# One forward substitution for both head groups of a gated delta rule, with the steps around it in another order

## The chip, the cores and the metric

The kernel runs on one core of a Trainium2 chip. The core has five engines that work through their own queues of instructions in order: TensorE (PE in the profile, for matmuls; PEld is its weight load), VectorE (DVE), ScalarE (ACT), GpSimd (POOL) and SyncE (SP, which issues the DMAs). An instruction waits on semaphores for what it needs from other engines, and everything behind it in the same queue waits with it. The metric is the device time of one launch in microseconds (us); smaller is better.

## What is computed

A decoder trunk of two layers on 512 tokens of width 1024. Layer 0 mixes tokens by a gated delta rule with six heads beside a cross-attention into 256 memory tokens; then follow an MLP, layer 1 (sliding-window attention) and its MLP. The change lies in layer 0 alone. The reference for it, cut:

```python
def gated_delta_rule(q, k, v, g, beta):
    ...
    L = jnp.where(strict, jnp.einsum('bhnid,bhnjd->bhnij', k_beta, k) * decay, 0.0)
    rhs = jnp.concatenate([v * beta[..., None], k_beta * jnp.exp(g)[..., None]], axis=-1)
    sol = lax.linalg.triangular_solve(L, rhs, left_side=True, lower=True, unit_diagonal=True)
    u, w = sol[..., :DV], sol[..., DV:]
    intra = jnp.where(incl, jnp.einsum('bhnid,bhnjd->bhnij', q, k) * decay, 0.0)
    ...
    def step(state, inp):
        qd, kd, uc, wc, ac, cd = inp
        v_new = uc - jnp.einsum('bhik,bhkv->bhiv', wc, state)
        out = jnp.einsum('bhik,bhkv->bhiv', qd, state) + jnp.einsum('bhij,bhjv->bhiv', ac, v_new)
        state = state * cd[..., None, None] + jnp.einsum('bhik,bhiv->bhkv', kd, v_new)
        return state, out

def mixer_a(h, mem, ...):
    proj = h @ w_in
    qkv = jax.nn.silu(causal_depthwise_conv(qkv, conv_w))
    ...
    o = gated_delta_rule(q, k, v, g, beta)
    o = o * lax.rsqrt(jnp.mean(o * o, axis=-1, keepdims=True) + NORM_EPS) * norm_w
    o = o * jax.nn.silu(z)
    mo = memory_cross_attention(qm, mem, mem_w_kv)
    return jnp.concatenate([o, mo], axis=-1) @ w_o
```

The kernel takes chunks of 128 tokens, so each head has 4 chunks. It needs, for each head and chunk, the inverse of a unit lower triangular matrix of 128 x 128.

## The kernel before

The six heads form two groups of three. The mixer of layer 0 is written as steps, each a function, and the string MIXER_ORDER lists them in the order in which they are written out; run_steps calls them. A letter is the step, the digits are its arguments. The tile framework then sets the final order of each engine's queue from the dependencies, so the order below shows what became of it.

The steps, with the lines of the kernel of before: q (proj_qm) is a projection. E (make_E1, from L339) makes a group's decay matrices: y on VectorE and on GpSimd (L346), two matmuls (L348), an Exp. k (group_kq) projects a head's k and q, runs a short convolution and a Silu over each (conv_silu: y on ScalarE at L356, three products on VectorE at L358, Silu at L360), and forms the products ak (L385) and from them LT, the triangular matrices. v (group_v) projects a head's v and runs the same convolution; w (group_v2) transposes it (vt, L430) and scales it (vr or TT, L431). z (proj_z) projects the gate z. Weights come through wload: a DMA into wr, a rounding cast wh on ScalarE (L87), the remainder wl on VectorE (L88), in few buffers. Most products are three f32r matmuls, of hi with hi, hi with lo and lo with hi.

i (inv_blocks) inverts the 32 x 32 diagonal blocks of a group's twelve matrices, in 48 rows of VectorE: the blocks go by DMA from LT to DRAM (dl, L442) and back with a block on each row (ld, L444), then 31 pairs of a product (tmp, L454) and a subtraction from X (L456), then X goes through DRAM (dx, L458) into TT (L461). j (inv_join) makes whole inverses from the blocks: transpose of TT into U (L467), products ipp, ip2, ip3 (copies Pf at L475 and L476), then iqp and iq for the 64 x 64 half. i and j run once for each group.

c (group_chunk) is a chunk of the scan for three heads: kt (a transpose of k), ks and qs (with the state S), R = v - ks on VectorE (L526), tr = U R (L532), vn, ds (L538, for the next state S), od. o (chunk_out) norms the chunk's output: sso, then f, with a power on GpSimd (L568), and a product with z in res (L573). n (z_norm) applies Silu to z (L657, ScalarE) and multiplies by the norm weights (L659, GpSimd). m is the memory attention in three parts, scores (msc), turn (mpt) and values (mov), which a pipeline (push, flush) spreads over later units. f (close_tile) transposes the mixed rows; W and p (wo_open, wo_tile) are the output projection; L (ln_tile) is the layer norm.

In before, both groups' steps interleave with projections as fillers: group 0 is inverted (i0, j0) while v and w are projected, its chunks c00 to c03 run among the v and w of group 1, and c10 to c13 among W and p.

Of the kernel before, what the change touches and what calls it, by code (L numbers as in the profile page):

```python
# [11 lines left out]
F32 = mybir.dt.float32  # L12
# [37 lines left out]
def trunk(ctx: ExitStack, tc: tile.TileContext, xT, xn, memT, wk, wq, wv, wqm, wz, wmk, wmv, wo0, wo1, up, dn,  # L50
# [47 lines left out]
    wa_stack = ExitStack()  # L98
    wpool[0] = wa_stack.enter_context(tc.tile_pool(name="wa", bufs=3))

    def feature_major(ps, w, mov_hi, mov_lo):
        hi, lo = w
        for k in range(KT):
            mh, ml = mov_hi(k), mov_lo(k)
            T.matmul(ps, hi[:, k, :], mh, start=(k == 0), stop=False)
            T.matmul(ps, hi[:, k, :], ml, start=False, stop=False)
            T.matmul(ps, lo[:, k, :], mh, start=False, stop=(k == KT - 1))

# [179 lines left out]
    def dt_(shape, tag, bufs=2, dt=F32):  # L288
        return dp.tile(shape, dt, tag=tag, name=nm(tag), bufs=bufs)
# [45 lines left out]
    GH = 3  # L335
    NU = GH * 4

    def make_E1(gi):
        E1 = dt_([P, NU, P], "E1")  # L339
        for hl in range(GH):  # L340
            h = GH * gi + hl
            ps = smt("E1")
            psv = ps.rearrange("p (c i) -> p c i", c=4)
            for i, eng in enumerate((V, G)):
                gm = dt_([P, 4, P], "y", dt=F32R)
                eng.tensor_tensor(gm, triu[:, :].unsqueeze(1).broadcast_to([P, 4, P]),  # L346
                                  fr(gsp[i])[:, h * 4:h * 4 + 4].unsqueeze(2).broadcast_to([P, 4, P]), op=ALU.mult)
                T.matmul(ps, slow, gm.rearrange("p c i -> p (c i)"), start=(i == 0), stop=(i == 1))  # L348
            dst = E1[:, hl * 4:hl * 4 + 4, :]
            V.tensor_tensor(dst, psv, mtri[:, :].unsqueeze(1).broadcast_to([P, 4, P]), op=ALU.add)  # L350
            A.activation(dst, dst, AF.Exp)
        E1s[gi] = E1

    def conv_silu(ps, ch, dst):
        y = dt_([P, 512], "y")
        A.activation(y, ps, AF.Identity, scale=convw[:, ch, 3:4])  # L356
        for s in (1, 2, 3):
            V.scalar_tensor_tensor(y[:, s:], ps[:, :512 - s], convw[:, ch, 3 - s:4 - s], y[:, s:],  # L358
                                   op0=ALU.mult, op1=ALU.add)
        A.activation(dst, y.rearrange("p (c i) -> p c i", c=4), AF.Silu)  # L360

    groups = {}
# [51 lines left out]
    def group_v(gi, hl):  # L414
        g = groups[gi]
        h = GH * gi + hl
        ps = mmt("v")
        feature_major(ps, wload(wv[h], [P, KT, P]), x_all(XH), x_all(XL))
        g["vt", hl] = dt_([P, 4, P], "vt")
        conv_silu(ps, 12 + h, g["vt", hl])  # L420

    def group_v2(gi, hl):
        g = groups[gi]
# [8 lines left out]
                        op=ALU.mult)  # L432

    Q = 4 * NU

    def inv_blocks(gi):

        LT = groups[gi]["LT"]
        dl = drp.tile([4, NU, 32, 32], F32, tag="dl", name=nm("dl"))
        for b in range(4):  # L440
            q = slice(32 * b, 32 * b + 32)
            SY.dma_start(dl[b].rearrange("u j i -> j u i"), LT[q, :, q])  # L442
# [4 lines left out]
        G.memset(X.rearrange("q i m -> q (i m)")[:, 0:1024:33], 1.0)
        tmp = dt_([Q, 256], "tmp", bufs=1)
        TT = groups[gi]["TT"] = dt_([P, NU, P], f"TT{gi}", bufs=1)
        G.memset(TT, 0.0)  # L450
        for j in range(31):
            n, m = 31 - j, j + 1
            tv = tmp[:, 0:n * m].rearrange("q (i m) -> q i m", m=m)
            V.tensor_tensor(tv, ld[:, j, j + 1:32].unsqueeze(2).broadcast_to([Q, n, m]),  # L454
                            X[:, j, 0:m].unsqueeze(1).broadcast_to([Q, n, m]), op=ALU.mult)
            V.tensor_sub(X[:, j + 1:32, 0:m], X[:, j + 1:32, 0:m], tv)  # L456
        dx = drp.tile([4, NU, 32, 32], F32, tag="dx", name=nm("dx"))
        SY.dma_start(dx.rearrange("b u i m -> (b u) (i m)"), X.rearrange("q i m -> q (i m)"))  # L458
        for b in range(4):
            q = slice(32 * b, 32 * b + 32)  # L460
            SY.dma_start(TT[q, :, q], dx[b].rearrange("u i m -> i u m"))  # L461

    def inv_join(gi):
        g = groups[gi]
        LT, TT = g["LT"], g["TT"]
        U = g["U"] = dt_([P, NU, P], "U")
        V.transpose(U.rearrange("p u i -> p (u i)"), TT.rearrange("p u i -> p (u i)"))  # L467

        b0, b1, b2, b3 = (slice(32 * b, 32 * b + 32) for b in range(4))
        pp = smt("ipp")[:, 0:NU * 32].rearrange("p (u i) -> p u i", u=NU)  # L470
        for u in range(NU):
            T.matmul(pp[b1, u, :], LT[b0, u, b1], TT[b0, u, b0], start=True, stop=True)
            T.matmul(pp[b3, u, :], LT[b2, u, b3], TT[b2, u, b2], start=True, stop=True)
        Pf = dt_([P, NU, 32], "Pf")
        A.copy(Pf[b1], pp[b1])  # L475
        V.tensor_copy(Pf[b3], pp[b3])  # L476
        p2 = smt("ip2")[:, 0:NU * 32].rearrange("p (u i) -> p u i", u=NU)
        p3 = smt("ip3")[:, 0:NU * 32].rearrange("p (u i) -> p u i", u=NU)
        for u in range(NU):
            T.matmul(p3[b1, u, :], U[b1, u, b1], Pf[b1, u, :], start=True, stop=True)  # L480
        for u in range(NU):
            T.matmul(p2[b0, u, :], Pf[b1, u, :], U[b1, u, b1], start=True, stop=True)
            T.matmul(p2[b2, u, :], Pf[b3, u, :], U[b3, u, b3], start=True, stop=True)
        V.tensor_scalar(TT[b1, :, b0], p3[b1], -1.0, None, op0=ALU.mult)
        A.activation(U[b0, :, b1], p2[b0], AF.Copy, scale=-1.0)
        V.tensor_scalar(U[b2, :, b3], p2[b2], -1.0, None, op0=ALU.mult)

        lo_, hi_ = slice(0, 64), slice(64, 128)
        for u0 in range(0, NU, 6):
            pp = smt("iqp")[:, 0:384].rearrange("p (u i) -> p u i", u=6)  # L490
            for u in range(6):
                T.matmul(pp[hi_, u, :], LT[lo_, u0 + u, hi_], TT[lo_, u0 + u, lo_], start=True, stop=True)
            P2 = dt_([P, 6, 64], "Pf")
            A.copy(P2[hi_], pp[hi_])
            p2 = smt("iq2")[:, 0:384].rearrange("p (u i) -> p u i", u=6)
            for u in range(6):
                T.matmul(p2[lo_, u, :], P2[hi_, u, :], U[hi_, u0 + u, hi_], start=True, stop=True)
            V.tensor_scalar(U[lo_, u0:u0 + 6, hi_], p2[lo_], -1.0, None, op0=ALU.mult)

    def group_chunk(gi, c):  # L500
        g = groups[gi]
        kq, vr, U, INT = g["kq"], g["vr"], g["U"], E1s[gi]
        if c == 0:
            g["S"] = dt_([P, GH, P], "S")
            g["scr"] = dt_([P, 4, GH, P], f"LT{gi}", bufs=1)
# [26 lines left out]
            T.matmul(tr[:, hl, :], U[:, hl * 4 + c, :], R[:, hl, :], start=True, stop=True)  # L532
        for hl in H:
            A.activation(vn[:, hl, :], tr[:, hl, :], AF.Copy, scale=col("brk", hl))
        if c < 3:
# [118 lines left out]
            features_half(src, t, j)  # L654

    def z_norm(t):
        A.activation(res[:, t, 0:768], res[:, t, 0:768], AF.Silu)  # L657
        zv = res[:, t, 0:768].rearrange("p (h d) -> p h d", h=NH)
        G.tensor_tensor(zv, zv, nw_b[:, :].unsqueeze(1).broadcast_to([P, NH, P]), op=ALU.mult)  # L659

    def mem0(t):
# [114 lines left out]
    def second_pools():  # L776
# [537 lines left out]
```

## Time and profile before

| | us |
|---|---|
| median of 3 runs (lowest to highest) | 1165.55 (1165.13 to 1166.28) |
| profiled execution | 1162.93 |
| its span, from the first to the last instruction | 1161.1 |
| TensorE busy in the span | 1132.5 |
| VectorE busy | 858.9 |
| ScalarE busy | 555.5 |
| GpSimd busy | 241.6 |

Times in a profile come from one execution, whose own time stands in the table's second line. Busy time of TensorE counts modelled ends of pipelined matmuls, so that one begins before the modelled end of the one before. A row of a timeline gives the start, the duration, engine, line, operation, out <- in, shape, and in brackets the idle time of the engine before it with what ended it. A row of the groups by line gives the count, busy time and mean of one in ns, idle time before. The granted clock of TensorE was 0.998 of full on the mean. The layer-0 mixer lies at some 42 to 300 us.

### The profile page before, as it was taken

How to read it: one execution, taken by the hardware profiler on the slowest of the kernel's cores; microseconds unless marked ns; L12 is line 12 of the kernel's file. 1: busy time of each engine (PE TensorE's matmuls, PEld its weight loads, DVE VectorE, ACT ScalarE, POOL GpSimd, SP SyncE). 2: the span in 40 equal slices, each digit the busy share in tenths (PEclk: the TensorE clock that was granted, in tenths of full speed). 3: DMA queues.
4: the chain of work that ended last, by engine and by line, in shares of the span. 5: the costliest groups of instructions: out<-in, count | busy, mean ns of one | idle time of the engine just before them, and what ended most of it. 6: DMA issues, size and time to landing. Idle time of an engine off the chain costs nothing.

```text
span 1161.1 us, 18955 instructions
## 1 busy us (share of the span) xinstructions
PE 1132.5 (98%) x7466; PEld 995.5 (86%) x7466; DVE 858.9 (74%) x1608; ACT 555.5 (48%) x1012; POOL 241.6 (21%) x180
## 2 busy tenths in 40 slices
PE   8999999989999999999999999999999999999996
PEld 8887788879998898998988877778988998989985
DVE  6678889876898666766665968886987666666657
ACT  6455355654574444454443336652654444444431
POOL 1212111110023423324220100000043324242204
PEclk9999999999999999999999999999999999999999
DMA  8423041205323232232324231102343232423311
GB/s 300 160 75 89 33 137 38 68 20 186 116 84 116 82 124 95 91 127 73 128 91 125 65 120 56 55 20 73 110 136 101 91 128 73 127 91 109 110 37 72
DMA packets 41016, 114.15 MB, mean 98 GB/s; under 512 B 11168, under 2 KB 12064, under 8 KB 40928
## 3 DMA queue, kind: packets, MB, share of 16 engines
q1 hardware_dynamic: 40352, 112.04, 30.0%
q8 instruction: 58, 0.95, 0.3%
q10 hardware_dynamic: 576, 0.92, 0.2%
q14 instruction: 30, 0.25, 0.1%
HBM read 109.53 MB, written 3.41 MB: 97 GB/s over the span
## 4 chain that ended last, share of the span: by engine, by line
PE 79%; DVE 14%; ACT 3%; issue 2%; POOL 1%; DMA 1%; SPq 0%; POOLq 0%; ACTq 0%; DVEq 0%
PE dn L116 9%; PE dn L115 9%; PE dn L117 9%; PE upb L918 3%; PE upb L920 3%; PE upb L919 3%; PE wo L115 2%; PE wo L117 2%; PE wo L116 2%; PE upd L920 2%; PE upd L919 2%; PE upd L918 2%; PE upa L919 2%; PE upa L918 2%; PE upa L920 2%; DVE y L358 2%
## 5 line engine op out<-in xcount | busy, mean ns | idle before, releaser
L87 ACT CAST wh<-wr 128x1024 fp32r<-128x1024 f32 (+1 forms) x126 | 132.2, 1052 | 216.4 <-PE dn L117 155.2
L88 DVE TENSOR_TENSOR wl<-wr,wh 128x1024 fp32r<-128x1024 f32 (+1 forms) x126 | 154.0, 1224 | 65.8 <-ACT wh L87 65.3
L115 PE MATMUL dn<-wh,hh 128*128 128x512 f32 x512 | 199.5, 390 | 0.0
L117 PE MATMUL dn<-wh,hl 128*128 128x512 f32 x512 | 199.4, 389 | 0.0
L116 PE MATMUL dn<-wl,hh 128*128 128x512 f32 x512 | 199.4, 389 | 0.0
L997 DVE TENSOR_TENSOR res<-res,dn 128x512 f32<-128x512 f32 x120 | 81.8, 682 | 44.0 <-PE dn L117 43.9
L117 PEld LDWEIGHTS dn<-wh,hl 128*128 128x128 f32 x512 | 96.1, 188 | 20.1
L115 PEld LDWEIGHTS dn<-wh,hh 128*128 128x128 f32 x512 | 96.1, 188 | 19.1
L116 PEld LDWEIGHTS dn<-wl,hh 128*128 128x128 f32 x512 | 96.1, 188 | 19.0
L908 POOL TENSOR_TENSOR sa<-wr 128x512 f32<-128x512 f32 x26 | 39.0, 1499 | 350.9 <-DMA wr<-in_up_dram 344.0
L696 POOL TENSOR_TENSOR rs<-rs,nhalf 128x1 f32<-128x1 f32 x16 | 13.4, 835 | 327.7 <-DVE rs L695 272.5
L918 PE MATMUL upb<-TH,wh 128*128 128x256 f32 x208 | 57.5, 277 | 1.5 <-DVE u L957 1.5
L919 PE MATMUL upa<-XL,wh 128*128 128x256 f32 x208 | 57.7, 277 | 0.0
L920 PE MATMUL upa<-XH,wl 128*128 128x256 f32 x208 | 57.5, 276 | 0.0
L919 PE MATMUL upb<-TL,wh 128*128 128x256 f32 x208 | 57.4, 276 | 0.0
L920 PE MATMUL upb<-TH,wl 128*128 128x256 f32 x208 | 57.4, 276 | 0.0
L918 PE MATMUL upd<-XH,wh 128*128 128x256 f32 x208 | 57.4, 276 | 0.0
L919 PE MATMUL upd<-XL,wh 128*128 128x256 f32 x208 | 57.4, 276 | 0.0
L920 PE MATMUL upd<-XH,wl 128*128 128x256 f32 x208 | 57.4, 276 | 0.0
L122 DVE TENSOR_TENSOR hl<-r,hh 128x1024 fp32r<-128x1024 f32 x26 | 56.0, 2153 | 1.9 <-ACT hh L121 1.9
L909 POOL TENSOR_TENSOR sb<-sa,wr 128x512 f32<-128x512 f32 x26 | 57.3, 2202 | 0.0
L121 ACT CAST wh<-wr 128x1024 fp32r<-128x1024 f32 x26 | 27.4, 1054 | 53.6 <-PE upa L919 53.6
(407 smaller groups left out, 3307.5 us busy)
## 6 DMA issues: line engine op xcount, KB each, us to landing
wr<-in_up_dram SPq DMA_DIRECT2D x64, 512.0 KB, 4.3
wr<-in_dn_dram SPq DMA_DIRECT2D x64, 512.0 KB, 4.2
wr<-in_wo_dram SPq DMA_DIRECT2D x16, 512.0 KB, 3.6
wr<-in_bw_dram SPq DMA_DIRECT2D x8, 512.0 KB, 4.5
wr<-in_wk_dram SPq DMA_DIRECT2D x6, 512.0 KB, 3.5
wr<-in_wq_dram SPq DMA_DIRECT2D x6, 512.0 KB, 4.3
wr<-in_wv_dram SPq DMA_DIRECT2D x6, 512.0 KB, 3.6
wr<-in_wz_dram SPq DMA_DIRECT2D x4, 520.0 KB, 4.2
```

Source lines behind the costliest of these rows:

```text
L87: A.copy(hi, raw)
L88: V.tensor_sub(lo, raw, fr(hi))
L115: T.matmul(ps, sh, hi[:, kk, :], start=(k == 0), stop=False)
L116: T.matmul(ps, sh, lo[:, kk, :], start=False, stop=False)
L117: T.matmul(ps, sl, hi[:, kk, :], start=False, stop=(k == nk - 1))
L122: return V.tensor_sub(lo, src, fr(hi))
L908: G.tensor_tensor(sa[:, 0], raw[1][:, kA], raw[1][:, kB], op=ALU.add)
L909: G.tensor_tensor(sb[:, 0], sa[:, 0], raw[0][:, kA], op=ALU.subtract)
L918: T.matmul(ps, hi[:, k, :], m, start=start and k == 0, stop=False, skip_group_check=True)
L919: T.matmul(ps, hi[:, k, :], ml[:, k, :], start=False, stop=False, skip_group_check=True)
L920: T.matmul(ps, lo[:, k, :], mh[:, k, :], start=False, stop=stop and k == 3, skip_group_check=True)
L997: V.tensor_tensor(dst, dst, ps, op=ALU.add)
```

## The change

One forward substitution takes both groups, in 96 rows (inv_blocks without an argument, step I). The gather (i) runs for each head right after its k step. E is made for each head. The join (j) takes both groups together. The v convolutions of heads 2 to 4 are pinned behind the last subtraction, that of head 5 behind the transpose of U, and the first matmul of v for head 5 behind the last ipp; behind() adds an order between two instructions without a semaphore of data. z_norm's Silu is pinned behind diag["copied"], the last copy of iqp. A chunk is split into c (up to vn) and d (group_state: ds, S, od, o), and both groups' chunks interleave; the memory unit's three parts are steps m, t and u of their own.

```diff
-MIXER_ORDER = """q0 g1 g0 E0 k02 k01 k00 E1 k12 i0 k10 k11 q1 z1 m3 v00 i1 m1 w00 v01 j0 m0 v02 w01 m2 z0 w02 M c00 v10 n0 o00
-c01 n1 v11 w10 o01 c02 n2 o02 j1 c03 v12 w11 w12 c10 n3 W1 W0 o03 o10 c11 f0 o11 c12 o12 f1 W3 c13 p10 p00 o13
-p01 f3 f2 X p11 p02 p12 p03 W2 p23 p20 p30 p32 p31 L0 p21 p13 p22 L1 L2 p33 L3"""
+MIXER_ORDER = """q0 g1 g0 E02 E01 k02 i02 E00 k01 i01 E12 k00 i00 E11 k12 i12 E10 k10 i10 k11 i11 q1 I z1 z0 v00 v01 v02 w00
+w01 v10 v11 w02 j w10 v12 w11 w12 W1 W0 c00 c10 n0 d00 m0 d10 n1 o00 c01 o10 t0 c11 n2 d01 u0 f0 d11 m1 o01 p10 c02 o11 t1 c12
+p00 d02 u1 f1 n3 d12 m2 o02 p11 c03 o12 t2 c13 p01 d03 u2 f2 d13 m3 o03 p12 o13 t3 p02 u3 f3 p13 p03 W3 X W2 p30 p31 p20 L0 p21
+p32 L1 p22 p33 L2 p23 L3"""
...
-            V.scalar_tensor_tensor(y[:, s:], ps[:, :512 - s], convw[:, ch, 3 - s:4 - s], y[:, s:],
-                                   op0=ALU.mult, op1=ALU.add)
+            behind(V.scalar_tensor_tensor(y[:, s:], ps[:, :512 - s], convw[:, ch, 3 - s:4 - s], y[:, s:],
+                                          op0=ALU.mult, op1=ALU.add), first)
...
-        feature_major(ps, wload(wv[h], [P, KT, P]), x_all(XH), x_all(XL))
+        feature_major(ps, wload(wv[h], [P, KT, P]), x_all(XH), x_all(XL), diag["ipp"] if h == 5 else None)
         g["vt", hl] = dt_([P, 4, P], "vt")
-        conv_silu(ps, 12 + h, g["vt", hl])
+
+        conv_silu(ps, 12 + h, g["vt", hl], None if h < 2 else diag["last"] if h < 5 else diag["U"])
...
+    def inv_gather(gi, hl):
...
+        dl = drp.tile([4, 4, 32, 32], F32, tag="dl", name=nm("dl"))
         for b in range(4):
             q = slice(32 * b, 32 * b + 32)
-            SY.dma_start(dl[b].rearrange("u j i -> j u i"), LT[q, :, q])
...
+            SY.dma_start(dl[b].rearrange("c j i -> j c i"), LT[q, hl * 4:hl * 4 + 4, q])
+        r = 16 * (GH * gi + hl)
+        SY.dma_start(diag["ld"][r:r + 16].rearrange("q j i -> q (j i)"), dl.rearrange("b c j i -> (b c) (j i)"))
...
-            V.tensor_tensor(tv, ld[:, j, j + 1:32].unsqueeze(2).broadcast_to([Q, n, m]),
-                            X[:, j, 0:m].unsqueeze(1).broadcast_to([Q, n, m]), op=ALU.mult)
-            V.tensor_sub(X[:, j + 1:32, 0:m], X[:, j + 1:32, 0:m], tv)
...
+            V.tensor_tensor(tv, ld[:, j, j + 1:32].unsqueeze(2).broadcast_to([2 * Q, n, m]),
+                            X[:, j, 0:m].unsqueeze(1).broadcast_to([2 * Q, n, m]), op=ALU.mult)
+            diag["last"] = V.tensor_sub(X[:, j + 1:32, 0:m], X[:, j + 1:32, 0:m], tv)
+        dxs = [drp.tile([4, NU, 32, 32], F32, tag="dx", name=nm("dx")) for _ in range(2)]
+        for gi in range(2):
+            for hl in range(GH):
+                r = 16 * (GH * gi + hl)
+                SY.dma_start(dxs[gi][:, hl * 4:hl * 4 + 4].rearrange("b c i m -> b c (i m)"),
+                             X[r:r + 16].rearrange("q i m -> q (i m)"))
...
+        for g in gs_:
+            U = g["U"] = dt_([P, NU, P], "U")
+            diag["U"] = V.transpose(U.rearrange("p u i -> p (u i)"), g["TT"].rearrange("p u i -> p (u i)"))
...
+                diag["ipp"] = T.matmul(pp[b3, u, :], LT[b2, u, b3], TT[b2, u, b2], start=True, stop=True)
+            Pf = g["Pf"] = dt_([P, NU, 32], "Pf")
+            A.copy(Pf[b1], pp[b1])
+            A.copy(Pf[b3], pp[b3])
...
+            diag["copied"] = A.copy(P2[hi_], pp[hi_])
...
+        g["open"] = kd, vn, o, None if c == 0 else qs
+
+    def group_state(gi, c):
...
-        A.activation(res[:, t, 0:768], res[:, t, 0:768], AF.Silu)
+        behind(A.activation(res[:, t, 0:768], res[:, t, 0:768], AF.Silu), diag["copied"])
...
-        push(mem_unit(dp, t, lambda j: res[:, t, 768 + j * P:768 + (j + 1) * P], KM[0], VM[0], res[:, t, :]))
+    def mem0(stage, t):
+        if stage == 0:
+            mem_units[t] = mem_unit(dp, t, lambda j: res[:, t, 768 + j * P:768 + (j + 1) * P], KM[0], VM[0], res[:, t, :])
+        mem_units[t][stage]()
```

The three places below show what became of the order. On VectorE, before, the second substitution (tmp and X at 48 rows) has the join of group 0 (U, Pf, ip, iq), weight remainders (wl) and the memory's maxima (mx) between its pairs:

```order
L88 TENSOR_TENSOR wl_2290<-wr_2287,wh_2289 128x1024
L456 TENSOR_TENSOR X_1719<-X_1719,tmp_1722 48x24x8
L467 STREAM_TRANSPOSE U_1869<-TT_161_1211 128x1536
L454 TENSOR_TENSOR tmp_1722<-ld_1717,X_1719 48x207
L476 COPY Pf_1896<-ipp_1871 32x384
L456 TENSOR_TENSOR X_1719<-X_1719,tmp_1722 48x23x9
L484 TENSOR_SCALAR TT_161_1211<-ip_249_1900 32x12x32
L454 TENSOR_TENSOR tmp_1722<-ld_1717,X_1719 48x220
L88 TENSOR_TENSOR wl_2385<-wr_2382,wh_2384 128x1024
L456 TENSOR_TENSOR X_1719<-X_1719,tmp_1722 48x22x10
L486 TENSOR_SCALAR U_1869<-ip_248_1899 32x12x32
```

Now the last pair of the one substitution, at 96 rows, stands right ahead of the convolutions of v02, v10 and v11 (three rows y each; wl is the remainder of a weight, vr a scaled v), and these ahead of the transpose into U. From the second row y of v02 on (lines of the changed kernel):

```order
L360 SCALAR_TENSOR_TENSOR y_1923<-v_1891,convw,y_1923 128x510
L360 SCALAR_TENSOR_TENSOR y_1923<-v_1891,convw,y_1923 128x509
L360 SCALAR_TENSOR_TENSOR y_1974<-v_1942,convw,y_1974 128x511
L89 TENSOR_TENSOR wl_2298<-wr_2295,wh_2297 128x1024
L360 SCALAR_TENSOR_TENSOR y_1974<-v_1942,convw,y_1974 128x510
L360 SCALAR_TENSOR_TENSOR y_1974<-v_1942,convw,y_1974 128x509
L434 TENSOR_TENSOR vr_1929<-vt_2018,rinv_681 128x512
L360 SCALAR_TENSOR_TENSOR y_2012<-v_1980,convw,y_2012 128x511
L89 TENSOR_TENSOR wl_2304<-wr_2301,wh_2303 128x1024
L360 SCALAR_TENSOR_TENSOR y_2012<-v_1980,convw,y_2012 128x510
L360 SCALAR_TENSOR_TENSOR y_2012<-v_1980,convw,y_2012 128x509
L485 STREAM_TRANSPOSE U_2024<-TT_202_1501 128x1536
```

So the convolutions moved from between the pairs to behind them, and U behind these.

On ScalarE the four copies of iqp (out ld and X, whose buffers they reuse) stand now ahead of the four z_norm Silus (res), a weight cast wh, and the last v's y and Silu:

```order
L515 COPY ld_2166<-iqp_2168 64x384
L515 COPY ld_2166<-iqp_2176 64x384
L515 COPY X_2167<-iqp_2184 64x384
L515 COPY X_2167<-iqp_2192 64x384
L689 ACTIVATE res<-res 128x768 x4
L88 CAST wh_2309<-wr_2307 128x1024
L358 ACTIVATE y_2271<-v_2239,convw 128x512
L362 ACTIVATE vt_2270<-y_2271 128x512
```

On TensorE the last matmuls of that v (v12) have the transposes vt behind them, v11's and v12's own, and then the scan's first rows:

```order
L109 MATMUL v_2239<-XL,wh_2242 128x512
L110 MATMUL v_2239<-XH,wl_2243 128x512
L433 MATMUL vt_2277<-ident,vt_2011 128x128 x4
L433 MATMUL vt_2283<-ident,vt_2270 128x128 x4
L538 MATMUL kt_2315<-ident,kq_679 128x128 x3
L555 MATMUL tr_2322<-vr_1929,U_2024 128x128 x3
L538 MATMUL kt_2331<-ident,kq_670 128x128 x3
```

The transpose of v12 (in vt_2270) stands right behind its last matmul and one other transpose, with no work between.

In the scan, on VectorE, the rows around R of chunk 2 (out LT, from ks at L549; LT_303 is group 0, LT_307 group 1). Ahead of it now stand the memory's maxima (mx), both groups' f rows of chunk 1 (L598 to L601), their products into res (L605), the output projection's eviction (L715) and the layer norm's statistics (st):

```order
L623 TENSOR_SCALAR mx_2540<-mx_2540 128x4
L599 TENSOR_SCALAR f_2556<-f_2556 128x3
L599 TENSOR_SCALAR f_2620<-f_2620 128x3
L601 TENSOR_TENSOR f_2556<-f_2556,rqs_686 128x3
L601 TENSOR_TENSOR f_2620<-f_2620,rqs_677 128x3
L605 SCALAR_TENSOR_TENSOR res<-LT_303_2314,f_2556,res 128x128 x3
L605 SCALAR_TENSOR_TENSOR res<-LT_307_2330,f_2620,res 128x128 x2
L715 SCALAR_TENSOR_TENSOR res<-res,wo_354_2564 128x256
L605 SCALAR_TENSOR_TENSOR res<-LT_307_2330,f_2620,res 128x128
L650 RECIPROCAL den_2541<-den_2541 128x4
L727 BN_STATS st_3240<-res 128x6
L549 SCALAR_TENSOR_TENSOR LT_303_2314<-ks_2597,gate_590,vr_1929 128x128 x3
```

In before, one group's f rows alone stood between two R; now both groups' stand ahead of the first group's R.

More of the change, by code (lines that the diff above doesn't have):

```diff
@@ L99, in trunk, with feature_major @@
     wpool[0] = wa_stack.enter_context(tc.tile_pool(name="wa", bufs=3))
-    def feature_major(ps, w, mov_hi, mov_lo):
+    def feature_major(ps, w, mov_hi, mov_lo, first=None):
         hi, lo = w
@@ L104, in feature_major @@
             mh, ml = mov_hi(k), mov_lo(k)
-            T.matmul(ps, hi[:, k, :], mh, start=(k == 0), stop=False)
+            m = T.matmul(ps, hi[:, k, :], mh, start=(k == 0), stop=False)
+            if k == 0:
+                behind(m, first)
             T.matmul(ps, hi[:, k, :], ml, start=False, stop=False)
@@ L463, in inv_join @@
[L463 to L467, printed above, removed]
-        b0, b1, b2, b3 = (slice(32 * b, 32 * b + 32) for b in range(4))
[L470 to L486, printed above, removed]
-        lo_, hi_ = slice(0, 64), slice(64, 128)
-        for u0 in range(0, NU, 6):
```

104 lines of the change are left out of this document (66 added, 38 removed).

## The prediction

> **What bounds the kernel now.** The page first: busy time by engine, then the chain of work that ended last.
>
> ```profile
> PE 1132.5 (98%) x7466; PEld 995.5 (86%) x7466; DVE 858.9 (74%) x1608; ACT 555.5 (48%) x1012; POOL 241.6 (21%) x180
> ...
> PE 79%; DVE 14%; ACT 3%; issue 2%; POOL 1%; DMA 1%; SPq 0%; POOLq 0%; ACTq 0%; DVEq 0%
> ```
>
> TensorE (PE) is the bound, and the change removes no matmul. It can gain only where PE stands still or where its stream gets cheaper. The table of busy time by stretch (PE, PEld, DVE, ACT, POOL, granted clock, DMA) shows how much of the layer-0 mixer stands still; its last line sums 60 to 320 us.
>
> ```profile
> 180.00:200.00 20.00, 18.63 (x164) 16.10 (x165) 18.68 (x38) 9.94 (x19) 3.90 (x2) 1.00 0.09 27
> 240.00:260.00 20.00, 17.04 (x196) 14.91 (x193) 14.02 (x38) 11.71 (x40) 2.55 (x3) 1.00 0.01 1
> sum 260.00, PE 249.70 PEld 217.38 DVE 209.71 ACT 135.42 POOL 34.53; mean PE 19.21 PEld 16.72 DVE 16.13 ACT 10.42 POOL 2.66
> ```
>
> PE stands 10.3 of those 260 us. Its modelled ends lie about 0.17 us behind the next start, so a stall is better measured from start to start: that way there are 20 stalls over 0.25 us from 50 to 320 us, 14.1 us together (10.3, 20 x 0.17, and two short ones before 60 us): 3.9 up to the end of q1 at about 140 us, 9.0 from 167 to 258 us, 1.3 in the layer norm. From that 14.1 the change can earn. The waits view (who waits for whom: us, times, longest) names the sources.
>
> ```profile
> PE vt L430 <- ACT vt L360: 2.4, 2, 1.9
> PE ak L385 <- ACT kq L360: 1.3, 2, 1.0
> PE E L348 <- POOL y L346: 1.3, 2, 1.1
> ```
>
> Each is a chain on other engines that PE reaches too early. The longest, in PE's timeline:
>
> ```profile
> 207.90 0.40 PE L107 MATMUL v<-XH,wl 128*128 128x512 f32 x1
> 208.13 0.39 PE L105 MATMUL v<-XH,wh 128*128 128x512 f32 x1
> 210.37 0.66 PE L430 MATMUL vt<-ident,vt 128*128 128x128 f32 x4 [1.85 <-ACT vt L360]
> ```
>
> PE issues a 512-wide matmul every 0.23 us (207.90 to 208.13) and then stands 1.85 us for the Silu of a value head, because its convolution shared VectorE (DVE) with the forward substitution:
>
> ```profile
> 185.47 2.09 DVE L454 TENSOR_TENSOR tmp<-ld,X 48x252 f32<-48x252 f32 x1
> 185.46 1.83 POOL L659 TENSOR_TENSOR res<-res,nw_b 128x768 f32<-128x768 f32 x1 [17.33 <-ACT res L657]
> ```
>
> A 0.42 us row took 2.09 us, as long as GpSimd's (POOL) z_norm multiply beside it. Four such rows, all beside the four multiplies, took 2.09, 1.97, 1.56 and 1.40 us.
>
> **The change part by part.** Prices of its operations (grouped by line: busy us, mean ns, idle before):
>
> ```profile
> L454 DVE TENSOR_TENSOR tmp<-ld,X 48x31 f32<-48x31 f32 (+15 forms) x62 | 24.2, 391 | 1.9 <-POOL X L447 1.2
> L456 DVE TENSOR_TENSOR X<-X,tmp 48x31 f32<-48x31 f32 (+15 forms) x62 | 22.0, 355 | 0.6
> L87 ACT CAST wh<-wr 128x1024 fp32r<-128x1024 f32 (+1 forms) x35 | 36.3, 1049 | 32.6 <-PE kq L106 13.7 <-DMA wr<-in_up_dram 6.9 <-PE wo L117 3.8
> L88 DVE TENSOR_TENSOR wl<-wr,wh 128x1024 fp32r<-128x1024 f32 (+1 forms) x35 | 42.6, 1223 | 8.2 <-ACT wh L87 8.1
> L356 ACT ACTIVATE y<-v,convw 128x512 f32<-128x512 f32 x6 | 4.1, 687 | 5.1 <-PE mov L615 4.9
> L358 DVE SCALAR_TENSOR_TENSOR y<-v,convw,y 128x511 f32<-128x511 f32 (+2 forms) x18 | 13.3, 739 | 1.0 <-ACT y L356 0.9
> L360 ACT ACTIVATE vt<-y 128x512 f32<-128x512 f32 x6 | 3.8, 631 | 8.0 <-DVE y L358 5.9 <-DVE f L567 2.1
> L467 DVE STREAM_TRANSPOSE U<-TT 128x1536 f32<-128x1536 f32 x2 | 3.5, 1767 | 0.0
> ```
>
> *One substitution at 96 rows.* 62 pairs become 31 pairs. The two groups cost 24.2 + 22.0 = 46.2 us of DVE; without the four long rows one costs 20.4. No row shows 96 rows in use; a row's length is set by its 31 to 256 elements, and if the row count cost in proportion the saving would be 0, so it is 0 to 25.8 us, and I take 25. It is DVE time beside PE work, so it earns nothing directly.
>
> *Up to the end of q1.* E is made per head, so GpSimd's y is issued a conv earlier, and ak has other work ahead. Of 3.9 us of stalls I keep 1.0 (0 to 3.9).
>
> *The join (S1).* The substitution must wait for the last head, and the join for the substitution. Its transfers:
>
> ```profile
> 217.40 0.34 SPq L458 DMA_DIRECT2D dx<-X  x1
> 221.24 1.86 SPq L461 DMA_DIRECT2D TT<-dx  x4
> TT<-dx SPq DMA_DIRECT2D x6, 48.0 KB, 2.3
> ld<-dl SPq DMA_DIRECT2D x1, 192.0 KB, 4.2
> ```
>
> I count time from the end of q1, t0. The last LT is written at t0+8.8. Four dl issues (1.9), their landing, and the ld (4.2 for three heads, now one) start the substitution at t0+15.5 (14.5 to 17). On DVE six convs, six wl and two vr stand among its pairs, some 12.6 us by the rows above, beside its own 20.4: it ends 33 us later, t0+48.5. X leaves in three issues a group and lands; before, dx to TT issue was 3.8, the four TT issues 1.9, landing 2.3, together 8.0; with two more issues 9, so TT of group 0 is there at t0+57.5. PE meanwhile has 192 z matmuls at 0.118 and 120 v matmuls at 0.233, 50.7 us, and 3.2 of small work and stalls (vt of v01, whose last conv stands 26.8 us into the substitution, waits 0.9, between 0 and 3.3): v11 ends at E = t0+54. From E: y 0.69; then a wh, 1.05, whose wl, 1.2, stands behind the first of v11's convs on DVE; two more convs 1.4; then the transpose of U, 1.77: ip3 at E+6.1. TT has landed by then, at E+3.6. PE has vt (0.45) and ipp (0.8) and nothing else, since v12 is pinned behind the last ipp: **4.85 us** of stall (4 to 6.5). If TT lands over 0.7 us later than this, S1 grows one for one.
>
> *The last v head (S2).* vt of v12 stands right behind v12 with one other vt (0.45). From v12's end: wh for W0 needs v12's slot and stands ahead of y on ScalarE (1.05), its wl ahead of the convs on DVE (1.13 start to start), three convs 2.1 (rows overlap by a little), Silu 0.63: 4.9 - 0.45 = 4.5. The four z_norm multiplies, 1.85 each, now follow diag["copied"] and run back to back from 3 us before v12's end to 4.5 us behind it. wl reads two SBUF tiles as the 2.09 us row does, so it waits for the running one: +1.65 (0 to 3.7). Together **6.15 us** (4.5 to 8.2).
>
> [...]
>
> *The scan.* Rows that stand ahead of R (the ks part) on DVE, and the step of a 256-wide matmul:
>
> ```profile
> L569 DVE TENSOR_TENSOR f<-f,rqs 128x3 f32<-128x3 f32 x8 | 1.3, 164 | 6.9 <-POOL f L568 6.9
> L590 DVE TENSOR_REDUCE mx<-msc 128x2 f32<-128x512 f32 x8 | 5.4, 679 | 0.0
> L573 DVE SCALAR_TENSOR_TENSOR res<-LT,f,res 128x128 f32<-128x128 f32 x24 | 7.1, 348 | 0.2
> L526 DVE SCALAR_TENSOR_TENSOR LT<-ks,gate,vr 128x128 f32<-128x128 f32 x9 | 2.9, 346 | 0.5 <-PE ks L524 0.5
> L679 DVE SCALAR_TENSOR_TENSOR res<-res,wo 128x256 f32<-128x256 f32 x16 | 6.7, 417 | 4.6 <-PE wo L117 4.3 <-DMA res<-in_xn_dram 0.3
> ```
>
> ```profile
> 6.02 0.28 PE L116 MATMUL VM<-wl,MH 128*128 128x256 f32 x1
> 6.14 0.28 PE L117 MATMUL VM<-wh,ML 128*128 128x256 f32 x1
> ```
>
> For c02 PE has, from the last od, msc 0.55, 24 wo0 at 0.12 = 2.9, kt, ks, qs 3 x 0.34: 4.5 us. DVE must first do two reduces 1.36, six small f rows 1.0, the pow wait 6.9/8 = 0.86, six res 1.76, one wo eviction 0.42, BN_STATS about 0.3, then R 0.87: 6.5. So tr waits **2.0**; c03 the same; c01, with little ahead of it but no wo0 either, 1.2; the second group's tr follows the first's R and waits 0.1, 0.4, 0.5. Sum 6.2 (3 to 9; one reason for 3 is that GpSimd's pow overlaps the reduces). Before, the groups' chunks stood apart, with v and w work between them.
>
> *Rest.* W3 and p30 0.3 (0 to 2.5), the layer norm 0.2 (L1 comes earlier, so 1.1 of its 1.3 goes), the join's other products 0.2 (0 to 1.6, what the two iq waits of before cost). The Pf copies move to ScalarE, which is busy under 60% of the time there; if it weren't, 0.47 more in S1.
>
> *Cheaper stream.* PE pays for going from the small f32 matmuls back to the f32r ones:
>
> ```profile
> 242.30 0.50 PE L105 MATMUL v<-XH,wh 128*128 128x512 f32 x1
> 242.63 0.40 PE L106 MATMUL v<-XL,wh 128*128 128x512 f32 x1
> ```
>
> The first 512-wide matmul after small ones takes 0.33 us to the next start instead of 0.23. By the order, such switches in the mixer fall from 116 to 64: 26 round trips less, at 0.09: **-2.3** (0 to -2.6).
>
> *Sum.* New stalls 1.0 + 0.9 + 4.85 + 6.15 + 6.2 + 0.3 + 0.2 + 0.2 = 19.8, against 14.1: +5.7; stream -2.3; net +3.4. The profiled execution took 1162.93 (span 1161.1 and 1.83 around it), 2.62 under the median of the runs. 1162.93 + 3.4 = 1166.3, or 1168.95 at the median: **1169.0**, its own range 1167.9 to 1171.5.
>
> **The rivals.**
> *A, faster.* DVE (VectorE), 25 us lighter, runs ahead, so that each new wait is only its own chain: nothing stands ahead of R (scan 1.5), wl is held by no multiply (S2 4.5), vt of the earlier head costs 0. Sum 1.0 + 4.85 + 4.5 + 1.5 + 0.7 = 12.55, less 14.1, less 2.3 = -3.9: 1161.7. It decides at R: if DVE reaches it within PE's 4.5 us, this is the case. For it: DVE was 18.68 of 20 us busy at 180 to 200. Against: the rows ahead of R stand in one queue with a wait inside.
>
> *B, no difference.* The new stalls come to 16.4 = 14.1 + 2.3, S1, S2 and the scan each a little shorter: 1163.3 to 1167.9.
>
> *C, the clock falls in the gap.* The stretches at the end of the trace:
>
> ```profile
> 1151.00:1152.00 1.00, 0.35 (x2) 0.00 (x0) 1.00 (x2) 0.72 (x1) 0.17 (x2) 1.00 0.00 0
> 1155.00:1156.00 1.00, 0.00 (x0) 0.00 (x0) 1.00 (x2) 0.42 (x1) 1.00 (x1) 0.82 0.00 0
> 1156.00:1157.00 1.00, 0.00 (x0) 0.00 (x0) 0.95 (x2) 0.20 (x1) 0.77 (x2) 0.50 0.00 0
> ```
>
> PE's last matmul ended at 1151.35, and the granted clock fell to 0.50 at 1155.64: 4.3 us idle. S2 is one gap of up to 6.15, S1 two of about 3.1 and 1.8. If S2 trips it, work runs at half speed until the clock is back. Before shows no return: a cost from 0 to that same 4.3 us at half speed, 2.15; the sum took 0, this case 2.15: 1171.1. Before's longest mixer gap is 1.85 us, and every stretch there was granted 1.00.
>
> [...]
>
> *D, a late join.* The first gather of before, from its first dl to the first pair:
>
> ```profile
> 106.33 2.80 SPq L442 DMA_DIRECT2D dl<-LT  x4
> 117.08 0.18 DVE L454 TENSOR_TENSOR tmp<-ld,X 48x31 f32<-48x31 f32 x1
> ```
>
> 10.7 us. If the last head takes as long, the substitution starts at t0+19.5, 4 us later, 0.7 of it slack: S1 +3.3; a second multiply ahead of wl adds 1.85. 1169 + 5.2 = 1174.2.
>
> *E, it doesn't do what it says*: the scheduler could undo the interleaving; the order shows 31 pairs at 96 rows and both groups' rows side by side in the scan, so it gets no chance of its own.
>
> **How the numbers follow.** Forecast 0.33, A 0.27, B 0.19, C 0.13, D 0.08. 0.2%, 2.3 us, is about what a measurement can tell from no change. Faster (under 1163.2) 0.27, same 0.19, slower 0.54. The range takes A's 1161.7 with 1.5 below it for larger gains, and D with a little above: 1160.2 to 1176, leaving out about 0.15. Signs differ between cases, hence the forecast's own range above.
>
> **What would show it.** 31 pairs of 0.39 + 0.36 us at 96 rows; a vt that waits 4 to 6 us for a Silu right behind v12, with a wl of over 2 us before it; an ip3 or ipp wait of some 5 us in two pieces before v12; tr waits of 2 us at R in c02 and c03; fewer stalls before q1. Wrong, if tr's waits together are under 2 us, if wl's row is 1.2, or if the mixer's PE idle sum falls below 10.3 us. A granted clock under 1.00 in the mixer means C.

## The result and the profile after

The changed kernel takes 1175.67 us (median of 4, 1174.85 to 1176.36), before beside it 1165.34: the ratio is 1.009, 95% interval 1.0076 to 1.0104. It is slower by about 10 us. That is some 7 us above the forecast of 1169.0, outside the forecast's own range (to 1171.5) and just under the top of the whole range (1176). The profiled execution took 1174.85, its span is 1173.1, 12.0 more than before. First the page's lines on the engines, the granted clock in 40 slices and the chain that ended last:

```profile
PE 1135.6 (97%) x7466; PEld 1001.6 (85%) x7466; DVE 840.4 (72%) x1544; ACT 555.8 (47%) x1014; POOL 238.8 (20%) x178
...
PEclk9999998899999999999999999999999999999999
...
PE 84%; DVE 9%; ACT 3%; DMA 2%; issue 1%; POOL 1%; SPq 0%; POOLq 0%; ACTq 0%; DVEq 0%
```

VectorE got 18.5 us lighter (858.9 to 840.4) and the kernel slower. The same 7466 matmuls took 3 us more of TensorE, and two slices of the clock are under 0.9 of full: the first sign that more than stalls is at work. TensorE's waits from 140 to 330 us (total, times, longest):

```profile
PE vt L433 <- ACT vt L362: 8.8, 2, 5.8
PE ip L501 <- ACT Pf L495: 4.9, 1, 4.9
PE tr L555 <- DVE LT L549: 3.6, 2, 1.8
...
PE tr L555 <- ACT p L627: 0.9, 1, 0.9
```

These are the waits the prediction listed: the two vt (v01 and v12), the join, and tr in the three chunks. The last row is chunk 1; the view puts its wait down to a row of the memory attention on ScalarE, but it goes in experiment 5 with those of the other chunks. Now the stretches just before and after each change of the clock (columns as in the table of before: PE, PEld, DVE, ACT, POOL, granted clock, DMA):

```profile
181.55:184.96 3.41, 0.52 (x5) 0.52 (x6) 3.34 (x9) 1.20 (x3) 0.00 (x0) 1.00 0.45 154
184.96:188.37 3.41, 3.41 (x11) 2.64 (x10) 3.31 (x9) 0.94 (x2) 0.00 (x0) 0.50 0.00 0
198.61:202.03 3.42, 0.46 (x28) 0.35 (x22) 3.38 (x5) 0.81 (x1) 0.00 (x0) 1.00 0.66 189
202.03:205.44 3.41, 1.49 (x40) 1.52 (x42) 1.78 (x2) 1.57 (x3) 0.00 (x0) 0.50 0.38 135
...
208.85:212.27 3.42, 3.42 (x9) 2.65 (x9) 0.58 (x1) 0.00 (x0) 0.00 (x0) 0.50 0.02 5
212.27:215.68 3.41, 3.41 (x99) 3.00 (x99) 1.10 (x2) 0.95 (x2) 0.00 (x0) 1.00 0.00 0
225.92:229.33 3.41, 0.00 (x0) 0.00 (x0) 3.17 (x4) 0.08 (x1) 0.00 (x0) 1.00 0.00 0
229.33:232.75 3.42, 2.81 (x13) 2.82 (x14) 0.69 (x1) 1.44 (x4) 0.00 (x0) 0.50 0.00 0
232.75:236.16 3.41, 3.41 (x31) 3.01 (x29) 1.12 (x2) 2.70 (x11) 0.00 (x0) 1.00 0.00 0
```

Each of the three long waits is followed by a stretch at half clock, of one, three and one times 3.413 us; all six changes lie on one grid of that step. A change from 1.00 to 0.50 is called a fall below. What half a clock does to one product, in TensorE's timeline:

```profile
184.86 0.68 PE L106 MATMUL v<-XH,wh 128*128 128x512 f32 x1
185.34 0.63 PE L109 MATMUL v<-XL,wh 128*128 128x512 f32 x1
185.76 0.63 PE L110 MATMUL v<-XH,wl 128*128 128x512 f32 x1
```

0.42 us from start to start instead of 0.23: a full window of such products (one step of the grid) loses, as an estimate from these two steps, about 1.55 us.

The 12.0 us come apart when every start on TensorE is set against the median step of its shape in the trace of before: stalls +9.35 (13.3 to 22.7, here those over 0.3 us; the prediction's 14.1 counts from 0.25 on), products at half clock +5.65 (0 to 5.65), cheaper stream -2.3, the rest of the program behind the first layer norm -2.7, and +2.0 in the first 20 us, where the two programs are the same. Of these 2.0 some 1.5 are a fall of the clock to 0.50 at 10.9 to 14.3 us. Four of the twelve other profiles of changed kernels have such a fall, the rest have none, so it isn't the change's; without the 2.0, 10.0 remain, and the medians say 10.3.

The substitution itself came out as forecast: 31 pairs at 96 rows, and a row takes no longer than at 48 rows (before: 391 and 355 ns on the mean, 24.2 + 22.0 us together):

```profile
L466 DVE TENSOR_TENSOR X<-X,tmp 96x31 f32<-96x31 f32 (+15 forms) x31 | 10.5, 338 | 0.8
L464 DVE TENSOR_TENSOR tmp<-ld,X 96x31 f32<-96x31 f32 (+15 forms) x31 | 10.4, 337 | 3.3 <-DMA ld<-dl 2.5
```

That saves 25.3 us, of which VectorE as a whole kept 18.5.

### The profile page after: what moved, and what is told of

It is laid out like the page before. It is cut to its first block, busy times and chain, and to the rows that moved or that the text cites. A ratio compares the mean times of both kernels' runs of the same rounds, so it can differ in the third digit from the quotient of the medians.

```text
span 1173.1 us, 18940 instructions
## 1 busy us (share of the span) xinstructions
PE 1135.6 (97%) x7466; PEld 1001.6 (85%) x7466; DVE 840.4 (72%) x1544; ACT 555.8 (47%) x1014; POOL 238.8 (20%) x178
## 3 DMA queue, kind: packets, MB, share of 16 engines
HBM read 109.53 MB, written 3.41 MB: 96 GB/s over the span
## 4 chain that ended last, share of the span: by engine, by line
PE 84%; DVE 9%; ACT 3%; DMA 2%; issue 1%; POOL 1%; SPq 0%; POOLq 0%; ACTq 0%; DVEq 0%
PE dn L119 9%; PE dn L118 9%; PE dn L120 9%; PE upb L955 3%; PE upb L956 3%; PE upb L957 3%; DVE wl L89 2%; PE upd L956 2%; PE upd L957 2%; PE upd L955 2%; PE upa L956 2%; PE upa L955 2%; PE upa L957 2%; PE wo L120 2%; PE wo L118 2%; PE up L110 2%
```

## The experiments

In the diffs, lines that only carry a handle to where it is needed are left out. Times are medians; each is also compared with the kernel before that ran beside it.

**1. Is the half clock a cost of its own?** TensorE gets work in the three waits that nobody reads.

```diff
+    def fill(n, after):
+        ps = smt("warm")
+        for _ in range(n):
+            m = T.matmul(ps, XH[:, 0, 0:P], XH[:, 0, :], start=True, stop=True)
+            behind(m, after)
+        return m
```

> Adds 50 matmuls of 128x512 whose result nobody reads, in the three long stalls of TensorE: 12 before the vt of v01, 18 between the first ipp and ip3, 20 before the vt of v12 (2.8, 4.2 and 4.7 us at 0.233, inside stalls of 3.2, 5.05 and 5.95). Theory: the three stretches at a granted clock of 0.50 cost time of their own (the first 1.55 us by 0.427 against 0.233 a matmul, the second some 3.5, the third some 1.2), so with TensorE kept busy the clock stays at 1.00 and the time falls by about 6, to 1169.5, while the stalls of the chains stay (last vt and ip3 at the same distance from the work ahead). Rival: the half clock lies beside waits of other engines and costs nothing; the stalls alone made the change slower: 1175.7 within 1.5.

1169.57 us (ratio 1.0035, 1.0017 to 1.0054), as the theory said. The profiled run was the fastest of ten (1166.27, granted clock 0.996); in it one of the three falls stayed. In the slowest, 1176.98, the granted clock was 0.987, as low as the changed kernel's: filling doesn't always hold it. The waits of the chains are still there, only filled. What is left of them to see is 1.3 in the join and 0.3 at vt; chunks 2 and 3 of the scan are unchanged:

```profile
PE tr L567 <- DVE LT L561: 3.6, 2, 1.8
PE ip L513 <- ACT Pf L505: 1.3, 1, 1.3
...
PE vt L441 <- ACT vt L363: 0.3, 1, 0.3
```

Fifty useless matmuls made the kernel some 5 us faster: about half of what the change lost was the clock.

**2. The pin of v12.**

```diff
-        feature_major(ps, ..., diag["ipp"] if h == 5 else None)
+        feature_major(ps, ..., None)
```

> Takes away the pin of v12's first matmul behind the last ipp, so v12 stands right behind v11's side work, ahead of ipp. Theory: S1 is idle because nothing may stand there; v12's 5.6 us fill its 5.05 us, and v12's convolutions and Silu then run beside the join, so the 5.95 us of S2 go too; waits inside the join that v12 covered come back, some 4 to 5. Net 5 to 6 us of stalls and two of the three clock falls: 1166 to 1170. Rival: the same wait moves into the join in full, since the join's own chain is what ends last: 1174 to 1176.

1168.67 (1.0026, 1.0012 to 1.004): inside the theory's range, but not by its sum. The 5.8 us vt wait of v12 is gone, and ip3 waits 3.0 and 2.0 for U instead of 4.9, as the theory had it. But where the theory took two falls away, the clock stayed at half from 201.98 to 225.87, 23.9 us, although TensorE waited less there. In the changed kernel it had come back behind a window that held v12's large products alone (208.85 to 212.27); here nothing large stands between the small ones, and the join runs at half clock throughout. By the sum above, stalls 22.7 to 14.9, the loss at half clock 5.65 to 8.5.

**3. The vt of v01.**

```diff
-... v00 v01 v02 w00 w01 v10 v11 w02 j ...
+... v00 v01 v02 v10 w00 w01 v11 w02 j ...
```

> Puts w00 and w01 behind v10 in the step order. Theory: vt of v01 waits 3.17 us only because it stands ahead of v10; behind it nothing waits, the clock fall right after goes too (1.55), v11 ends 4.7 us earlier; ip3 then waits for TT, which lands at 197.9 and makes U ready at 199.7 instead of 203.8, so about 4 of the 4.7 are kept: 1171 to 1172.5. Rival: the join is bound by the substitution and its transfers, S1 grows by what vt loses: 1175 to 1176.

1173.74 (1.0064, 1.0042 to 1.0086), against 1174.77 (1.0072) of the changed kernel run again below and 1175.67 (1.009) at first: 1 to 2 us, not 4, and not clear of the noise. TensorE's waits at the join:

```profile
PE ip L501 <- ACT Pf L495: 3.9, 1, 3.9
...
PE ipp L491 <- DMA TT<-dx: 1.8, 2, 1.5
```

vt of v01 no longer waits (3.0 before), but ipp now waits 2.0 for the DMA of TT, and ip3 3.9 instead of 4.9. So S1 grew by 1.0 of the 3.0, and the truth lies between the two: part of what v01 saves is waited for at the substitution's transfers. The fall behind v01 is gone, but the one at S2 lasted two windows in this profile instead of one, so the half clock cost as much as before.

**4 and 5. The scan.** First only the step order, then with a pin.

```diff
-... d11 m1 o01 p10 c02 o11 t1 c12 ...
+... d11 m1 p10 c02 o01 t1 c12 o11 ...
```

> Puts each o step (f rows with the GpSimd power, three res products) behind the next chunk's c of its group. Theory: the tr waits of 1.03, 2.05 and 1.94 us come from the f and res rows ahead of R on VectorE; behind R they hold nobody, tr's waits fall to 2 us together: 1172 to 1173. Rival: R waits for the chain ds, S, ks itself, or the shift takes work from where it covered the chunk, so tr waits as long: 1175 to 1177.

1172.72 (1.0058), inside the band, but not for the reason: tr waited 4.0 in three places where it had waited 4.5. In chunks 2 and 3 the scheduler had put f and res ahead of R again (the rows R stands behind, at 251 to 254 us, are the same), so nothing follows on the theory from its time. What went in its profile is the first fall, with a wait for vt of v01 of 1.5 instead of 3.0.

```diff
+... d11 m1 p10 c02 t1 c12 o01 o11 ...
-        V.tensor_mul(f, sso, cc(g["rq2"]))
+        behind(V.tensor_mul(f, sso, cc(g["rq2"])), diag.get(("R", c + 1)))
```

> As the changed kernel, with the o steps of a chunk written behind both c steps of the next one, and their first f row on VectorE pinned behind the last row R of the next chunk, so that f and res stand behind R there, which the step order alone did not bring for chunks 2 and 3. Theory (the f and res rows ahead of R make tr wait): tr's waits of chunks 1 to 3, 5.0 us together, fall to 2 or less, the time by about 3, to 1172.7 or less. Rival: R was waited for because of the state's chain or of the memory's maxima, or the rows moved back come up as a wait of to_feapt for res: tr plus to_feapt still 4 to 5, 1174.5 to 1176.

1170.36 (1.004, 1.0025 to 1.0055). TensorE's waits from 225 to 280 us:

```profile
PE to_feapt L679 <- DVE S L575: 0.5, 1, 0.5
PE tr L555 <- DVE LT L549: 0.3, 1, 0.3
```

With f and res behind R, tr waits 0.3 instead of 4.5, and 0.5 come up at to_feapt. The cause of the scan's waits is shown. Experiment 4, whose profile has the same first half, is the fairer measure of the time: 2.4 us.

**6 and 7. Real work in the gaps, and both.** v12 ahead of the first ipp, w00 and w01 behind v10, both U ahead of the join's products, the wl of W1 and W0 behind U, z_norm's Silus later; then the scan's pin too.

```diff
+            behind(diag["ipp0"], mm_last[0])      # at v12
-        V.tensor_sub(lo, raw, fr(hi))
+        behind(V.tensor_sub(lo, raw, fr(hi)), first)
-            V.tensor_scalar(TT[b1, :, b0], p3[b1], -1.0, None, op0=ALU.mult)
+            behind(V.tensor_scalar(TT[b1, :, b0], p3[b1], -1.0, None, op0=ALU.mult), diag["U"])
```

> As the changed kernel, with the three long stalls filled by work of the kernel: w00 and w01 behind v10; v12 ahead of the first ipp; both transposes into U ahead of the products of the join on VectorE; the casts of W1 and W0 behind them; z_norm's Silus no longer ahead of v12's Silu. Theory: TT lands at about 198 and U needs 1.8 us; v12 covers that; the stalls of 3.2, 5.05 and 5.95 fall to 3 together, and of the 5.65 us at half clock at most one window (some 1.6) stays: 22.7 - 11 and 4 less, 1160 to 1163. Rival: the join's chain is the bound whatever stands beside it: 1166 or more, no better than v12 alone moved (1168.7).

> The filled join and the scan with f and res behind R together. Theory: the two gains add, 1157 to 1160, below the kernel before. Rival: what the scan saves is waited for elsewhere: as the filled join alone.

Both 1163.91 (0.9978, 0.9969 to 0.9987, and 0.9984, 0.9974 to 0.9994): some 0.2% faster than before, less than was expected, and they don't add. In the first the three long stalls are down to 0.7 + 0.6 at the join, and the new longest is 2.3 (ks behind the kd rows on ScalarE). The clock takes the rest: four windows at half, beginning where TensorE hardly waited:

```profile
197.91:201.32 3.41, 2.90 (x99) 2.34 (x99) 3.32 (x3) 2.26 (x4) 0.00 (x0) 1.00 0.02 5
201.32:204.74 3.42, 2.86 (x159) 2.71 (x151) 1.65 (x4) 1.42 (x3) 0.00 (x0) 1.00 0.02 5
204.74:208.15 3.41, 3.41 (x36) 3.41 (x33) 2.05 (x3) 1.43 (x3) 0.00 (x0) 0.50 0.02 5
208.15:211.56 3.41, 3.41 (x39) 3.41 (x38) 0.52 (x1) 0.95 (x2) 0.00 (x0) 0.50 0.00 0
```

The window ahead of the fall is 84% busy, but all but one of its matmuls are of 32 x 32 (ip, ipp); the next two hold those of 64 x 64 and don't bring the clock back. In the second, what the scan saved came up as a wait of to_feapt for VectorE, with another fall behind it:

```profile
PE to_feapt L683 <- DVE S L579: 2.8, 1, 2.8
PE ks L551 <- ACT LT L544: 1.0, 1, 1.0
```

**8 and 9. The price of z_norm beside wl.** A pin of the multiplies on GpSimd behind a row of VectorE, and then the Silus that feed them later on ScalarE.

```diff
-        G.tensor_tensor(zv, zv, ...)
+        behind(G.tensor_tensor(zv, zv, ...), diag["cv"])
```

> As the changed kernel, with GpSimd's four z_norm multiplies behind the last convolution of v12. Theory (wl waits for the running multiply): the wl that took 2.14 us there takes 1.22, and vt of v12 waits 5.0 instead of 5.95. Rival: the row was long for another reason (ScalarE's cast beside it, the clock): 2.1 stays.

The multiplies stood where they had stood (7.2 us from 212.28 on, wl 2.14), though the row they were pinned behind comes only at 222: the pin did nothing, and this is the changed kernel once more, at 1170.53 in one run.

```diff
-        behind(A.activation(res[:, t, 0:768], res[:, t, 0:768], AF.Silu), diag["copied"])
+        behind(A.activation(res[:, t, 0:768], res[:, t, 0:768], AF.Silu), diag["z", 0])
```

> As the changed kernel, with the four z_norm Silus on ScalarE behind v12's Silu, so that GpSimd's multiplies, which wait for them, run behind the wl of W0. (The pin of the multiplies themselves in the run before moved nothing: it orders one engine's own queue and the instruction it named is on another.) Theory, a wl that reads two SBUF tiles waits for a running multiply: that wl takes 1.2 us instead of 2.14, vt of v12 waits 5.0 instead of 5.95. Rival, the row is long for another reason: 2.1 and 5.95 stay. The Silus then stand ahead of the scan's first rows on ScalarE and cost up to 3 there, so the time of the run tells nothing by itself.

The row in the changed kernel, and the multiplies beside it:

```profile
224.80 2.14 DVE L89 TENSOR_TENSOR wl<-wr,wh 128x1024 fp32r<-128x1024 f32 x1
...
218.67 7.18 POOL L691 TENSOR_TENSOR res<-res,nw_b 128x768 f32<-128x768 f32 x4 [72.30 <-ACT res L689]
```

and with the Silus later:

```profile
230.75 1.22 DVE L89 TENSOR_TENSOR wl<-wr,wh 128x1024 fp32r<-128x1024 f32 x1
...
PE vt L433 <- ACT vt L362: 4.9, 1, 4.9
```

1.22 and 4.9: the multiply cost 0.92 us of S2. In the changed kernel the last multiply ended at 225.85, and wl 1.09 later, so nearly all of wl ran after it. The whole took 1181.84 in one run, whose profile lost 14.8 us to half clock, more than twice the changed kernel's 5.65.

**10 to 12. The clock in the join, and the changed kernel again.**

```diff
+            fill(3, diag["ipp"])      # behind ipp of each group
+                fill(3, m)            # behind ip2 of the second group
+                fill(4, m)            # behind the last iqp
```

> The changed kernel itself once more, beside the others, since profiles of kernels that share its first half showed the wait for vt of v01 at 1.6 to 1.8 us instead of 3.2, and the clock fall behind it missing. If that first fall comes and goes with the time of the gather: 1171 to 1174, a little under the first 1175.7; if 1175.7 was its usual time: 1175 to 1176.5.

> The filled join with the scan's f rows behind R, and 13 matmuls of 128x512 whose result nobody reads, 3 or 4 at each of four places among the small matmuls of the join (32x32 and 64x64). Theory: the clock counts a stretch of such small matmuls as idle although TensorE's row is full (it fell at the end of a stretch of 3.4 us with 147 of them and 84% busy, and before kept it with 4 large ones in such a stretch): it stays at 1.00, the 9.0 us at half clock go but for one window, the 13 cost up to 3.0: 1156 to 1159.5. Rival: the clock fell because of the waits inside the join, or needs full rows of large matmuls: half clock as before and 1163.9 + 1 to 3.

> The same with close_tile of tile 0 behind the second group's d step, since to_feapt waited 2.8 us for rows on VectorE ahead of its input, and a clock fall followed. Theory: that wait shrinks to 1 or less: 1.5 to 2.5 under the kernel with the 13 matmuls alone. Rival: it moves to the wo matmuls that need the features: the same time.

The changed kernel again: 1174.77 (1171.18 to 1176.73; ratio 1.0072, 1.0057 to 1.0088). Its runs spread by 5.5 us, and its profile shows the first fall again, so neither of the two answers holds alone: the fall is usual, not constant.

Thirteen useless matmuls in the join of experiment 7: 1160.92, **0.9957 of before (0.9945 to 0.9969)**, the best of the study, though over the expected 1156 to 1159.5. Its profiled run was the fastest of six (1158.06). In it the clock holds through the join, in stretches as full of small products as the ones above:

```profile
199.95:203.36 3.41, 3.41 (x148) 3.00 (x146) 1.31 (x3) 1.09 (x3) 0.00 (x0) 1.00 0.02 5
203.36:206.78 3.42, 3.42 (x48) 3.01 (x49) 3.32 (x5) 1.70 (x4) 0.00 (x0) 1.00 0.02 5
```

The variant with close_tile later:

```diff
-... n2 d01 u0 f0 d11 m1 ...
+... n2 d01 u0 d11 f0 m1 ...
```

It took 1162.04 (0.9964, 0.9952 to 0.9977) and gained nothing: to_feapt's wait moved, as its rival had it, but to ds (2.7) and not to the wo matmuls. Its profiled run was the slowest of six (1169.34, granted clock 0.985; the others 1161.01 to 1163.37, at 0.992 to 0.994). In it the clock fell all the same, behind a window almost like the one above:

```profile
203.51:206.92 3.41, 3.41 (x147) 3.30 (x147) 1.70 (x4) 1.09 (x3) 0.00 (x0) 1.00 0.02 5
206.92:210.34 3.42, 3.42 (x28) 2.79 (x28) 3.14 (x4) 0.55 (x2) 0.00 (x0) 0.50 0.02 5
```

Both windows held two of the added matmuls and 144 of ip. So two among that many of 32 x 32 kept the clock in one run and lost it in another; what decided isn't shown, the grid's place, which differs from run to run, being the nearest guess. More of them were not tried. Nor is it the count of large products alone. In the profile of experiment 1 a window of 61 matmuls of 32 x 32 and 38 of 64 x 64, with no large one, kept the clock:

```profile
205.79:209.20 3.41, 3.41 (x103) 3.37 (x102) 1.11 (x2) 1.43 (x3) 0.00 (x0) 1.00 0.02 5
209.20:212.62 3.42, 3.42 (x48) 2.94 (x46) 0.72 (x2) 3.05 (x5) 1.18 (x1) 1.00 0.00 0
```

## Why the prediction held, and where it was off

The direction was right, and so was the mechanism that the forecast named: new waits outweigh the ones that went. It made a little over half of the loss. The rest was rival C, the clock, on top of the forecast. That the time still lies inside the range is luck in part: the range's top came from D, a late join, and what filled that room was mostly the clock. By terms, forecast and measured in the profiled execution (start to start, as the prediction counted):

| term | forecast | measured |
|---|---|---|
| stalls up to q1 | 1.0 | 1.3 |
| vt of v01 | 0.9 | 3.2 |
| join, S1 | 4.85 | 5.05 |
| last v head, S2 | 6.15 | 5.95 |
| scan (tr) | 6.2 | 5.0 |
| stream | -2.3 | -2.3 |
| clock | 0 | +5.65 |
| behind the first layer norm | 0 | -2.7 |

- *Stalls.* Their sum (19.8 with the small terms, measured 22.7) is right but for one: vt of v01 came out near the upper end of its range of 3.3. Its Silu waited for a convolution that shares VectorE with wl and the pairs, and the sum had the pairs start too early: 15.5 us behind the last product of q1, where the first pair came at 17.8 (156.37 against 138.6), halfway to D's 19.5. In the profiles with the same first half, a first pair at 15.9, 16.3, 17.8 and 18.0 goes with 1.2, 1.7, 3.2 and 3.4 us of this stall (experiments 2 and 4, the changed kernel, experiment 9), so it moves with the gather; what moves the gather stays open.
- *S1.* The size is right; the last link was another. ip3 waited for the Pf copy on ScalarE, which stands behind v11's Silu, and ended at 203.85, level with U at 203.8:

```profile
203.38 0.47 ACT L495 COPY Pf<-ipp 32x384 f32<-32x384 f32 x1
202.04 1.77 DVE L485 STREAM_TRANSPOSE U<-TT 128x1536 f32<-128x1536 f32 x1
```

- *S2.* Right in sum, the parts less so: the multiply held wl 0.92, not 1.65, and the hand-overs and y made it up. Experiment 9 showed the part.
- *Scan.* 1.0, 2.05 and 1.9 for the forecast 1.2, 2.0 and 2.0, and the cause shown by experiment 5; the second group's small waits of 0.1 to 0.5 did not come.
- *The clock is the step that failed.* The sum took the cost of the fall as 0 and made it a rival of 2.15 for S2 alone. All three gaps tripped it: the gap of 3.0 at vt, which the prediction had at 0.9 and not on C's list, S1's of 4.9, and S2's of 5.8. The end of before's trace (4.3 us idle, then 0.50) was read as a threshold on a single gap. On the grid of 3.413 us each of the three falls came at the end of a window that held little: busy 0.52, 0.46 and 0.00 of 3.41 us. Windows full of small products were followed by a fall as well, busy 2.86 of 3.42 us in experiment 6 and 3.41 of 3.41 in 12, so the busy time alone doesn't tell when it falls. Experiment 1 prices the clock at some 5 us of the 10.
- *Not in the sum.* The rest of the program behind the layer norm got 2.7 us shorter, for which the prediction had no term; it hid part of the clock's cost. Its cause isn't shown.

What was gained where it was expected: less VectorE work and a cheaper stream. It could not be cashed in, because VectorE is not the bound and the join now stands in one piece, with little that is large beside it. With work in the gaps, the f rows behind R and the clock kept up, the same merged substitution is 0.43% faster than before (experiment 11, with its 13 useless matmuls).

## What to carry to other kernels

Price a new wait of TensorE twice: as the wait, and as the half clock that can follow. Here one, three and one windows of 3.41 us at 0.50 stood behind the three long waits and cost 5.65 us beside 14.2 us of such waits. Work that is merged into one stretch loses what used to stand between its pieces; look at what is left beside it, on the bound engine first. A pin without a semaphore that names an instruction on another engine ordered nothing (experiment 8), and a step order is no order of rows: see where they stand before a run is read.

## What the hardware showed beyond that

- Matmuls of 32 x 32 and 64 x 64 left TensorE's row full and the clock at half in experiment 6: with 146 of 32 x 32 and one of 64 x 64 in a window, busy for 2.86 of 3.42 us, the clock fell, and windows of 3.41 us busy with 31 and 36 of 64 x 64 didn't bring it back. In the trace of before a window with four large products among some 90 small ones (237.46 to 240.88 us) kept 1.00, and in experiment 1 one with 38 of 64 x 64 among 61 of 32 x 32 did. What decides stays open; busy time in a profile doesn't, since before also kept 1.00 in and behind a window busy for 2.69 of 3.41 us (240.88 to 244.29).
- VectorE rows with two inputs in SBUF took longer beside a running GpSimd multiply: the same wl 2.14 us, of which 1.09 lay behind the multiply's end, against 1.22 without one (experiment 9), and in before four rows of the substitution 2.09, 1.97, 1.56 and 1.40 us against 0.40, 0.36, 0.30 and 0.40 for rows of the same shapes elsewhere in that trace. Rows beside it with an input in PSUM did not: y 0.73 (before), U from iq 0.55 (the changed kernel, and 0.55 without a multiply in experiment 9).
- A VectorE row of the substitution took no longer at 96 rows than at 48: 0.34 us on the mean against 0.36 to 0.39, where before had four rows beside multiplies.
- The clock fell in the first 15 us, where the programs are alike, in one profile and not in the other (10.9 to 14.3 us at 0.50 in the changed kernel's, at 1.00 in before's): 1.5 us of difference that no edit made. The profile of before was one of the best of its kind: its granted clock was 0.998, while 53 of the 54 runs of before beside the experiments had 0.992 to 0.997.
